# A hybrid decoder block on one core: input norm by products with a diagonal, and a norm weight that is a scale by channel

## The chip, the cores and the metric

The kernel runs on one core of a Trainium2 chip. The metric is the device time of one execution in microseconds (us). A core has five engines with an instruction stream each, which run in order and wait for each other by semaphores: TensorE (PE in the profile; its weight loads are PEld), VectorE (DVE), ScalarE (ACT), GpSimd (POOL) and SyncE (SP), which here issues nearly all transfers. Data lie in an on-chip memory of 128 partitions; TensorE's results go to eight PSUM banks of 128 x 512 float32.

## The reference

One decoder block on 512 tokens of 1024 channels, float32. Only the beginning matters here:

```
u    = rmsnorm(x, norm_mix_pre_w)        # x * rsqrt(mean(x*x) + 1e-6) * w, by token
proj = u @ w_in                          # 1024 x 10528
q, k, v, z, xbc, dt_raw, gate_logits = split(proj)
```

Then come a dilated attention on q, k and v, a Mamba-2 mixer on z, xbc and dt, projections of both that are merged by gates, an output projection, and an MLP with squared ReLU, each with residuals and norms. All of that is the same in both kernels.

## The kernel before, in words

Every large product is made of three products in a reduced float32 format: each operand is split into a high part, which ScalarE copies, and a low part, which VectorE (or GpSimd) gets by subtraction; then high x high, high x low and low x high are added up in PSUM (`three`, line 229). So a weight piece needs a transfer into `ws`, a ScalarE pass into `wh` and a VectorE or GpSimd pass into `wl` before TensorE can use it.

The start of the kernel (lines 272 to 424) makes the normed input `u`, transposed so that channels lie on partitions, in high parts `uh` and low parts `ul`, and from it the values v and the step sizes dt. x is taken in four blocks of 128 tokens (i = 0 to 3). For a block, `square_u` squares it on ScalarE with a sum by token, VectorE adds epsilon, and GpSimd takes the power of -0.5 (`rs`, one number for each token). `norm_u` multiplies x by `rs` and by the norm weight on VectorE; the weight lies in `row0`, one row that a transfer repeats over all 128 partitions. `transpose_u` turns eight 128x128 pieces on TensorE into two PSUM banks, and `split_u` makes the high and the low parts.

The values are 768 columns, taken in three groups d of 256 columns, in the order d = 1, 0, 2; group 0 has the 32 columns of dt with it and so 288. `values(d, i)` is one such group for one block: eight steps k over the channels, three products each, all into one bank `psv`; then ScalarE copies it to `vtok`. The table `V_STEPS` says what is put in behind step k of `values(d, i)`: "s" is `square_u`, "n" is `norm_u`, "t" the transposes and the split of a block, "w" the split of the weights of group 0, "p" the weights of group 2.

Most of these instructions are pinned, so they stand on their engine in the order in which the program names them. The others (the splits of later weights, the copies to `vtok`, three scalings of constants `cw`, `cb` and `bg` on GpSimd at line 400) are put among them by a scheduler. SyncE issues its transfers in the order of the program; a transfer's semaphore is used again eight transfers later, so a late issue can wait for an earlier landing. From line 425 on the order is the same in both kernels.

Of the kernel before, what the change touches and what calls it, by code (L numbers as in the profile page):

```python
# [11 lines left out]
F32 = mybir.dt.float32  # L12
F32R = mybir.dt.float32r
AF = mybir.ActivationFunctionType
ALU = mybir.AluOpType
# [3 lines left out]
P = 128  # L19
# [58 lines left out]
def hybrid_block(ctx: ExitStack, tc: tile.TileContext, a: dict):  # L78
# [193 lines left out]
    with tc.tile_pool(name="start", bufs=1, reuse_waits="tile") as st:  # L272
        VW = UC + SH
        row0 = st.tile([P, D], F32, name="row0")
        xt = st.tile([P, NT, D], F32, name="xt")
# [6 lines left out]
        def load_x(i):  # L282
            for cs in (slice(0, T), slice(T, D)) if i == 0 else (slice(0, D),):
                sp.dma_start(xt[:, i, cs], a["x"][0, i * P : (i + 1) * P, cs])

        def load_row(cs):
            sp.dma_start(row0[:, cs], a["norm_mix_pre_w"][:, cs].broadcast_to([P, T]))
# [14 lines left out]
        sp.dma_start(ws0[:, :, UC:], w_in[:, :, OFF_DT : OFF_DT + SH])  # L302
        ssq = st.tile([P, NT], F32, name="ssq")
        sq0 = st.tile([P, 2], F32, name="sq0")
        rs = st.tile([P, NT], F32, name="rs")
        uns, pts = {}, {}

        def square_u(i):
            un = uns[i] = st.tile([P, D], F32, name=f"un{i}", tag="un", bufs=2)
            if i == 0:  # L310
                for n, cs in enumerate((slice(0, T), slice(T, D))):
                    pin(act.activation(un[:, cs], xt[:, i, cs], AF.Square, scale=RD, accum_out=sq0[:, n : n + 1]))
                pin(dve.tensor_scalar(rs[:, i : i + 1], sq0[:, 0:1], sq0[:, 1:2], EPS, ALU.add, ALU.add))
            else:
                pin(act.activation(un, xt[:, i, :], AF.Square, scale=RD, accum_out=ssq[:, i : i + 1]))
                pin(dve.tensor_scalar(rs[:, i : i + 1], ssq[:, i : i + 1], EPS, None, ALU.add))
            pin(pool.tensor_tensor(rs[:, i : i + 1], rs[:, i : i + 1], mhalf, op=ALU.pow))

        def norm_u(i):
            for cs in (slice(0, T), slice(T, D)):  # L320
                pin(dve.scalar_tensor_tensor(uns[i][:, cs], xt[:, i, cs], rs[:, i : i + 1], row0[:, cs],
                                             op0=ALU.mult, op1=ALU.mult))

        def transpose_u(i, b):
            pt = pts[i, b] = abank(f"ut{i}_{b}")
            for j in range(4):
                k = 4 * b + j
                tr(pt[:, j * P : (j + 1) * P], uns[i][:, k * P : (k + 1) * P])

        def split_u(i, b):  # L330
            p3 = pts.pop((i, b)).rearrange("p (k t) -> p k t", k=4)
            hi = uh[:, 4 * b : 4 * b + 4, i * P : (i + 1) * P]
            pin(act.activation(hi, p3, AF.Copy))
            pin(dve.tensor_tensor(ul[:, 4 * b : 4 * b + 4, i * P : (i + 1) * P], p3, hi.bitcast(F32), op=ALU.subtract))

# [5 lines left out]
        def split_v0(k, eng=dve):  # L341
            ks = slice(k, k + 4)
            pin(act.activation(wh0[:, ks, :], ws0[:, ks, :], AF.Copy))
            pin(eng.tensor_tensor(wl0[:, ks, :], ws0[:, ks, :], wh0[:, ks, :].bitcast(F32), op=ALU.subtract))
# [12 lines left out]
        for j, n in enumerate(("dt_bias", "a_log")):  # L357
# [22 lines left out]

        norm_u(1)
        wv = {1: (v3(wh1, KD), v3(wl1, KD))}
        for d, i in V_ORDER:
            for k, _ in enumerate(values(d, i)):
                for step, n in V_STEPS.get((d, i, k), ()):
                    if step == "t":
                        transpose_u(n, 0)
                        transpose_u(n, 1)
                        split_u(n, 0)
                        split_u(n, 1)  # L390
                    elif step == "w":
                        split_v0(0)
                        split_v0(4, pool)
                    elif step == "p":
                        prep(0, 0)
                        wv[2] = [v3(t, KD) for t in take("v2")]
                    else:
                        (square_u if step == "s" else norm_u)(n)
        for t in (cw, cb_, bg):
# [713 lines left out]
```

## Time and profile before

| | |
|---|---|
| median of 3 runs | 1108.72 us (1108.58 to 1109.34) |
| the profiled execution | 1109.38 us, its span 1107.6 us |
| PE busy | 1089.4 us, 98% of the span |
| DVE, ACT, POOL busy | 663.0, 489.5, 63.5 us |
| first transposes, first product of the values | 7.78 us, 11.02 us |
| TensorE's idle time ahead of transposes of the input norm | 9.4 us in three waits |

Times in the rows that follow are us from the start of the span. A row of a timeline gives the start, the duration, the engine, the line of the kernel, the operation, what it writes and reads, the shape, how many instructions the row merges, and in brackets how long the engine sat idle before it and what ended that. Rows of TensorE overlap, since products are pipelined: the spacing of their starts is what one costs. In lists of waits come the time in total, the number of waits and the longest.

### The profile page before, as it was taken

To read this page: it belongs to the slowest core of one execution; us is meant where nothing else is said; L and a number is where in the kernel's file an instruction comes from. 1 tells how busy PE (TensorE), PEld (TensorE's weight loads), DVE (VectorE), ACT (ScalarE), POOL (GpSimd) and SP (SyncE) were. 2 spreads that over 40 slices of the span, in tenths; PEclk is the share of its full clock that TensorE was granted. 3 is DMA by queue.
4 is the path that set the end of the run, shared out by engine and by line. 5 is a ranking of instruction groups with operands and counts; after the bars stand their busy time and mean duration, and the time that the engine had idled before them with its cause. 6 is when DMAs were issued, how large, how long until landed. Compare 5 with 4: busy or idle time off the path is not lost.

```text
span 1107.6 us, 13600 instructions
## 1 busy us (share of the span) xinstructions
PE 1089.4 (98%) x5501; PEld 906.4 (82%) x5501; DVE 663.0 (60%) x978; ACT 489.5 (44%) x835; POOL 63.5 (6%) x71
## 2 busy tenths in 40 slices
PE   6999999999999999999999999999999999999997
PEld 5988887778878888888888888889888888888886
DVE  5657666446776869696969695865423234332324
ACT  6346656445375654637373723454322324232321
POOL 2203122000000000000000000000000000000000
PEclk9999999999999999999999999999999999999999
DMA  8232122323323232332423233540333233323212
GB/s 274 81 100 83 56 70 67 105 67 105 114 76 115 77 114 77 114 103 88 140 84 120 77 86 105 200 142 12 118 100 104 86 114 133 114 77 114 77 37 76
DMA packets 86463, 110.86 MB, mean 100 GB/s; under 512 B 4080, under 2 KB 74224, under 8 KB 85376
## 3 DMA queue, kind: packets, MB, share of 16 engines
q1 hardware_dynamic: 85072, 101.01, 28.4%
q0 software_dynamic: 1328, 8.98, 2.2%
q8 instruction: 43, 0.70, 0.3%
q14 instruction: 20, 0.16, 0.1%
HBM read 107.81 MB, written 2.16 MB: 99 GB/s over the span
## 4 chain that ended last, share of the span: by engine, by line
PE 94%; ACT 2%; DVE 2%; issue 1%; DMA 1%; SPq 0%; POOL 0%; POOLq 0%; DVEq 0%; ACTq 0%
PE psu L221 16%; PE psd L221 15%; PE psz L221 8%; PE pssp L221 8%; PE psx L221 8%; PE psbc L221 6%; PE psga L221 4%; PE psgs L221 4%; PE psk L221 3%; PE psq L221 3%; PE psv L221 3%; PE psap L221 3%; PE psp L221 2%; PE pso L221 2%; PE pq L221 1%; PE pyd L221 1%
## 5 line engine op out<-in xcount | busy, mean ns | idle before, releaser
L221 PE MATMUL psu<-fh,wh_up 128*128 128x512 f32 (+1 forms) x288 | 105.4, 366 | 0.0
L221 PE MATMUL psu<-fl,wh_up 128*128 128x512 f32 (+1 forms) x288 | 105.2, 365 | 0.0
L221 PE MATMUL psu<-fh,wl_up 128*128 128x512 f32 (+1 forms) x288 | 105.2, 365 | 0.0
L221 PE MATMUL psd<-wl_dn,hh 128*128 128x512 f32 x240 | 93.4, 389 | 0.0
L221 PE MATMUL psd<-wh_dn,hl 128*128 128x512 f32 x240 | 93.4, 389 | 0.0
L221 PE MATMUL psd<-wh_dn,hh 128*128 128x512 f32 x240 | 93.4, 389 | 0.0
L93 DVE TENSOR_TENSOR wl_up<-ws_up,wh_up 128x2048 fp32r<-128x2048 f32 x16 | 36.7, 2292 | 77.6 <-ACT wh_up L90 77.4
L93 DVE TENSOR_TENSOR hl<-hidden,hh 128x512 fp32r<-128x512 f32 x32 | 21.9, 693 | 77.3 <-ACT hh L90 77.2
L90 ACT ACTIVATE hh<-hidden 128x512 fp32r<-128x512 f32 x32 | 20.2, 632 | 103.1 <-PE psd L221 97.6
L221 PEld LDWEIGHTS psu<-fl,wh_up 128*128 128x128 f32 x288 | 54.3, 189 | 8.8
L221 PEld LDWEIGHTS psu<-fh,wh_up 128*128 128x128 f32 x288 | 54.3, 189 | 8.7
L221 PEld LDWEIGHTS psu<-fh,wl_up 128*128 128x128 f32 x288 | 54.3, 189 | 8.7
L90 ACT ACTIVATE wh_up<-ws_up 128x2048 fp32r<-128x2048 f32 x16 | 30.7, 1916 | 61.3 <-PE psu L221 56.1
L221 PE MATMUL psbc<-uh,wh_bc 128*128 128x512 f32 x128 | 52.8, 413 | 0.0
L221 PEld LDWEIGHTS psd<-wh_dn,hh 128*128 128x128 f32 x240 | 45.1, 188 | 9.5
L221 PEld LDWEIGHTS psd<-wl_dn,hh 128*128 128x128 f32 x240 | 45.1, 188 | 9.5
L221 PEld LDWEIGHTS psd<-wh_dn,hl 128*128 128x128 f32 x240 | 45.1, 188 | 9.2
L221 PE MATMUL pssp<-yth,wh_sp 128*128 128x512 f32 x128 | 51.3, 401 | 0.0
L221 PE MATMUL psz<-uh,wh_z 128*128 128x512 f32 x128 | 51.1, 399 | 0.0
L221 PE MATMUL psx<-uh,wl_x 128*128 128x512 f32 x128 | 49.9, 390 | 0.7 <-DVE wl_x L93 0.7
L221 PE MATMUL psx<-uh,wh_x 128*128 128x512 f32 x128 | 50.5, 394 | 0.0
L221 PE MATMUL psz<-uh,wl_z 128*128 128x512 f32 x128 | 50.2, 392 | 0.2 <-DVE wl_z L93 0.2
(271 smaller groups left out, 2786.1 us busy)
## 6 DMA issues: line engine op xcount, KB each, us to landing
ws_up<-in_w_up_dram SPq DMA_DIRECT2D x16, 1024.0 KB, 5.4
ws_dn<-in_w_down_dram SPq DMA_DIRECT2D x15, 1024.0 KB, 5.0
ws_z<-in_w_in_dram SPq DMA_DIRECT2D x8, 1024.0 KB, 7.3
ws_x<-in_w_in_dram SPq DMA_DIRECT2D x8, 1024.0 KB, 5.2
w<-acs_d POOLq DMA_DIRECT2D x8, 1024.0 KB, 6.1
ws_bc<-in_w_in_dram SPq DMA_DIRECT2D x16, 512.0 KB, 4.6
ws_sp<-in_w_ssm_proj_dram SPq DMA_DIRECT2D x8, 1024.0 KB, 5.0
ws_ga<-in_w_in_dram SPq DMA_DIRECT2D x4, 1024.0 KB, 5.3
```

Source lines behind the costliest of these rows:

```text
L90: ins = act.activation(hi, src, AF.Copy)
L93: ins = (eng or dve).tensor_tensor(lo, src, hi.bitcast(F32), op=ALU.subtract)
L221: tc.keep_in_program_order(pe.matmul(*args, **kw))
```

## The change

The norm weight is no longer a row on all partitions but a column: `ncol` holds it as 128 x 8, channel on partition, sent by ScalarE's queue. The transposes become true products: x itself is the stationary operand and the moving one is a diagonal of `rs` (`diag_u`, identity times `rs` by token on VectorE), so the product transposes and scales by token at once. `norm_u` is gone. The norm weight is then a scale by partition on the transposed rows: for blocks 1 to 3 and the second half of block 0 `split_u` has an added VectorE pass into `un` that multiplies by `ncol`, ahead of the high and the low part; for the first half of block 0 `split_u0` takes the channel pieces one by one and has the scale in ScalarE's copy and in VectorE's subtraction. For blocks 0 and 1 the second half of the squares is a VectorE instruction that multiplies and sums (`tensor_tensor_reduce`). Block 1 of x is sent in halves, behind the first weight piece instead of behind the last. Ahead of all stand 24 products of ones with ones into a bank that nobody reads. In the table, the squares of block 2 move from behind step 2 of the first group to behind the transposes of block 1, and the "n" steps fall away; the diagonals of blocks 2 and 3 are made right ahead of their transposes.

```diff
-V_STEPS = {(1, 0, 2): (("s", 2),), (1, 0, 5): (("t", 1),), (1, 0, 6): (("n", 2),), (1, 1, 1): (("s", 3),),
-           (1, 1, 3): (("t", 2),), (1, 1, 5): (("n", 3),), (1, 2, 3): (("t", 3), ("w", 0)), (1, 2, 7): (("p", 0),)}
+V_STEPS = {(1, 0, 5): (("t", 1), ("s", 2)), (1, 1, 1): (("s", 3),),
+           (1, 1, 3): (("t", 2),), (1, 2, 3): (("t", 3), ("w", 0)), (1, 2, 7): (("p", 0),)}
+WARM = 24
...
-        load_row(slice(0, T))
+        act.dma_start(ncol, a["norm_mix_pre_c"])
         for k in range(0, KD, 2):
             sp.dma_start(v3(ws1, KD)[:, k : k + 2, :], w_in[:, k : k + 2, OFF_V + UC : OFF_V + 2 * UC])
             if k == 0:
-                load_row(slice(T, D))
-            if k == KD - 2:
                 load_x(1)
...
         def square_u(i):
+            jk = st.tile([P, D], F32, name=f"jk{i}", tag="jk", bufs=2)
+            if i < 2:
+                pin(act.activation(jk[:, :T], xt[:, i, :T], AF.Square, scale=RD, accum_out=ssq[:, i, 0:1]))
+                pin(dve.tensor_scalar(ssq[:, i, 1:2], ssq[:, i, 0:1], EPS, None, ALU.add))
+                pin(dve.tensor_tensor_reduce(jk[:, T:], xt[:, i, T:], xt[:, i, T:], 1.0 / D, ssq[:, i, 1:2], ALU.mult,
+                                             ALU.add, rs[:, i : i + 1]))
...
+        def diag_u(i):
+            dgs[i] = st.tile([P, P], F32, name=f"dgu{i}", tag="dgu", bufs=2)
+            pin(dve.tensor_scalar(dgs[i], ident, rs[:, i : i + 1], None, ALU.mult))
+
+        def transpose_u(i, b, banks=1):
...
-                tr(pt[:, j * P : (j + 1) * P], uns[i][:, k * P : (k + 1) * P])
+                mm(pts[i, b][0][j], xt[:, i, k * P : (k + 1) * P], dgs[i], start=True, stop=True)
 
         def split_u(i, b):
...
+            pin(dve.tensor_tensor(un, p3, ncol[:, ks].unsqueeze(2).broadcast_to([P, 4, P]), op=ALU.mult))
+            hi = uh[:, ks, ts]
+            pin(act.activation(hi, un, AF.Copy))
+            pin(dve.tensor_tensor(ul[:, ks, ts], un, hi.bitcast(F32), op=ALU.subtract))
+
+        def split_u0(k):
+            pk = pts[0, 0][0][k]
+            hi = uh[:, k, 0:P]
+            pin(act.activation(hi, pk, AF.Copy, scale=ncol[:, k : k + 1]))
+            pin(dve.scalar_tensor_tensor(ul[:, k, 0:P], pk, ncol[:, k : k + 1], hi.bitcast(F32), op0=ALU.mult,
+                                         op1=ALU.subtract))
...
+        warm = gbank("warm")
+        for _ in range(WARM):
+            mm(warm[:, 0:P], ones, ones, start=True, stop=True)
         square_u(0)
-        norm_u(0)
         split_v1(0)
-        transpose_u(0, 0)
+        diag_u(0)
+        transpose_u(0, 0, 2)
         transpose_u(0, 1)
-        split_v1(2, pool)
-        split_u(0, 0)
-        split_v1(4)
+        square_u(1)
+        split_u0(0)
+        split_u0(1)
+        split_v1(2)
+        split_u0(2)
+        split_u0(3)
+        split_v1(4, pool)
         split_u(0, 1)
         split_v1(6)
-        square_u(1)
+        diag_u(1)
...
                     if step == "t":
+                        if n > 1:
+                            diag_u(n)
                         transpose_u(n, 0)
```

The order of the instructions moves at three places of which the prediction speaks. Numbers behind a name are those of the buffer; a 0 or 1 ahead of it is the half of the block. `rs` is the addition or the power, `un` the normed rows (before) or the scaled transposed half (now), `jk` what the squares leave, `dgu` the diagonal, `vtok` the copy of a finished group.

VectorE from block 1 to block 2, before:

```order
L316 TENSOR_SCALAR rs<-ssq 128x1
L321 SCALAR_TENSOR_TENSOR un_153<-xt,rs,row_98 128x512 x2
L316 TENSOR_SCALAR rs<-ssq 128x1
L334 TENSOR_TENSOR ul<-ut_0_200,uh 128x4x128
L334 TENSOR_TENSOR ul<-ut_1_205,uh 128x4x128
L321 SCALAR_TENSOR_TENSOR un_187<-xt,rs,row_98 128x512 x2
```

The same place now:

```order
L319 TENSOR_SCALAR dgu_191<-ident,rs 128x128
L333 TENSOR_TENSOR un_0_240<-ut_00_230,ncol 128x512
L336 TENSOR_TENSOR ul<-un_0_240,uh 128x4x128
L333 TENSOR_TENSOR un_1_244<-ut_10_235,ncol 128x512
L336 TENSOR_TENSOR ul<-un_1_244,uh 128x4x128
L314 TENSOR_SCALAR rs<-ssq 128x1 x2
L319 TENSOR_SCALAR dgu_276<-ident,rs 128x128
```

The addition for block 2 stood ahead of block 1's low parts; now the additions for blocks 2 and 3 stand together behind them, and block 2's diagonal behind both.

ScalarE at the same place, before:

```order
L315 ACTIVATE un_153,ssq<-xt 128x1024
L315 ACTIVATE un_187,ssq<-xt 128x1024
L333 ACTIVATE uh<-ut_0_200 128x4x128
L333 ACTIVATE uh<-ut_1_205 128x4x128
L377 ACTIVATE vtok<-psv_0_177 128x256
L315 ACTIVATE un_230,ssq<-xt 128x1024
```

And now:

```order
L335 ACTIVATE uh<-un_0_240 128x4x128
L438 ACTIVATE rows<-rows 128x32
L393 ACTIVATE vtok<-psv_0_211 128x256
L335 ACTIVATE uh<-un_1_244 128x4x128
L313 ACTIVATE jk_248,ssq<-xt 128x1024
L313 ACTIVATE jk_266,ssq<-xt 128x1024
L335 ACTIVATE uh<-un_0_288 128x4x128
```

The squares of blocks 1 and 2 stood ahead of block 1's high parts and those of block 3 behind them; now the squares of blocks 2 and 3 both stand behind the two high parts of block 1 and the copy of the first group.

GpSimd from the first power on, before:

```order
L317 TENSOR_TENSOR rs<-rs,mhalf 128x1
L339 TENSOR_TENSOR wl_v_109<-ws_v_107,wh_v_108 128x512
L317 TENSOR_TENSOR rs<-rs,mhalf 128x1 x3
L400 TENSOR_SCALAR cw<-cw 128x128
L400 TENSOR_SCALAR cb<-cb 128x32
L400 TENSOR_SCALAR bg<-bg 128x16
L344 TENSOR_TENSOR wl_v_102<-ws_v_100,wh_v_101 128x1152
```

And now:

```order
L315 TENSOR_TENSOR rs<-rs,mhalf 128x1 x2
L348 TENSOR_TENSOR wl_v_109<-ws_v_107,wh_v_108 128x512
L417 TENSOR_SCALAR cw<-cw 128x128
L417 TENSOR_SCALAR cb<-cb 128x32
L315 TENSOR_TENSOR rs<-rs,mhalf 128x1
L417 TENSOR_SCALAR bg<-bg 128x16
L315 TENSOR_TENSOR rs<-rs,mhalf 128x1
L353 TENSOR_TENSOR wl_v_102<-ws_v_100,wh_v_101 128x1152
```

All four powers stood ahead of the scalings of the constants; now `cw` and `cb` are scaled ahead of block 2's power, and `bg` ahead of block 3's.

VectorE between blocks 2 and 3 now (before, the two halves of `wl_v` of group 2 stood behind all low parts of block 3):

```order
L333 TENSOR_TENSOR un_0_288<-ut_00_278,ncol 128x512
L336 TENSOR_TENSOR ul<-un_0_288,uh 128x4x128
L333 TENSOR_TENSOR un_1_292<-ut_10_283,ncol 128x512
L95 TENSOR_TENSOR wl_v_361<-ws_v_358,wh_v_360 128x1024
L336 TENSOR_TENSOR ul<-un_1_292,uh 128x4x128
L319 TENSOR_SCALAR dgu_322<-ident,rs 128x128
L95 TENSOR_TENSOR wl_v_361<-ws_v_358,wh_v_360 128x1024
```

One half of group 2's low part is now ahead of block 2's last low part and of block 3's diagonal, the other right behind that diagonal. ScalarE's two high halves of that weight have moved with them.

More of the change, by code (lines that the diff above doesn't have):

```diff
@@ L273, in hybrid_block @@
         VW = UC + SH
-        row0 = st.tile([P, D], F32, name="row0")
+        ncol = st.tile([P, KD], F32, name="ncol")
         xt = st.tile([P, NT, D], F32, name="xt")
@@ L282, in load_x @@
         def load_x(i):
-            for cs in (slice(0, T), slice(T, D)) if i == 0 else (slice(0, D),):
+            for cs in (slice(0, T), slice(T, D)) if i < 2 else (slice(0, D),):
                 sp.dma_start(xt[:, i, cs], a["x"][0, i * P : (i + 1) * P, cs])
-        def load_row(cs):
-            sp.dma_start(row0[:, cs], a["norm_mix_pre_w"][:, cs].broadcast_to([P, T]))
         load_x(0)
@@ L302, in hybrid_block @@
         sp.dma_start(ws0[:, :, UC:], w_in[:, :, OFF_DT : OFF_DT + SH])
-        ssq = st.tile([P, NT], F32, name="ssq")
-        sq0 = st.tile([P, 2], F32, name="sq0")
+        ssq = st.tile([P, NT, 2], F32, name="ssq")
         rs = st.tile([P, NT], F32, name="rs")
-        uns, pts = {}, {}
+        pts, dgs = {}, {}
         def square_u(i):
[L309 to L313, printed above, removed]
-            else:
-                pin(act.activation(un, xt[:, i, :], AF.Square, scale=RD, accum_out=ssq[:, i : i + 1]))
-                pin(dve.tensor_scalar(rs[:, i : i + 1], ssq[:, i : i + 1], EPS, None, ALU.add))
+            jk = st.tile([P, D], F32, name=f"jk{i}", tag="jk", bufs=2)
[4 more added lines that the diff above has]
+                                             ALU.add, rs[:, i : i + 1]))
+            else:
+                pin(act.activation(jk, xt[:, i, :], AF.Square, scale=RD, accum_out=ssq[:, i, 0:1]))
+                pin(dve.tensor_scalar(rs[:, i : i + 1], ssq[:, i, 0:1], EPS, None, ALU.add))
@@ L326, in transpose_u @@
+        def transpose_u(i, b, banks=1):
+            pt = [abank(f"ut{i}_{b}{n}") for n in range(banks)]
+            pts[i, b] = [pt[j % banks][:, j * P : (j + 1) * P] for j in range(4)], pt[0]
             for j in range(4):
                 k = 4 * b + j
-                tr(pt[:, j * P : (j + 1) * P], uns[i][:, k * P : (k + 1) * P])
+                mm(pts[i, b][0][j], xt[:, i, k * P : (k + 1) * P], dgs[i], start=True, stop=True)
         def split_u(i, b):
-            p3 = pts.pop((i, b)).rearrange("p (k t) -> p k t", k=4)
@@ L397, in hybrid_block @@
                     else:
-                        (square_u if step == "s" else norm_u)(n)
+                        square_u(n)
         for t in (cw, cb_, bg):
@@ L1096 @@
     data["conv_b"] = data["conv_b"][0].reshape(32, P).T
+    data["norm_mix_pre_c"] = data["norm_mix_pre_w"][0].reshape(8, P).T
     data["b_gate"] = data["b_gate"][0].reshape(16, P).T
```

13 lines of the change are left out of this document (3 added, 10 removed).

## The prediction

> **What bounds the kernel now.** I read the page first, then the list of waits of TensorE, then the timeline of each engine over the first 32 us.
>
> ```profile
> span 1107.6 us, 13600 instructions
> PE 1089.4 (98%) x5501; PEld 906.4 (82%) x5501; DVE 663.0 (60%) x978; ACT 489.5 (44%) x835; POOL 63.5 (6%) x71
> PEclk9999999999999999999999999999999999999999
> ```
> ```profile
> PE ut L224 <- DVE un L321: 9.4, 3, 7.8
> PE pyd L221 <- DVE w L764: 0.8, 2, 0.6
> PE psx L221 <- DVE wl_x L93: 0.7, 1, 0.7
> PE rg L221 <- ACT dg L819: 0.6, 1, 0.6
> ```
>
> TensorE (PE) is the bound: 1089.4 of 1107.6 us. The waits worth naming sum to 11.5 us, and 9.4 of them are the three before transposes of the input norm, which is what is changed. So whatever the start loses or gains reaches the end of the kernel: behind it only 2.1 us of waits are left that could swallow a delay.
>
> ```profile
> 7.78 1.11 PE L224 MATMUL ut<-ident,un 128*128 128x128 f32 x4 [7.78 <-DVE un L321]
> 9.97 1.12 PE L224 MATMUL ut<-ident,un 128*128 128x128 f32 x4 [1.08 <-DVE un L321]
> 11.02 0.58 PE L221 MATMUL psv<-wh_v,uh 128*128 128x256 f32 x1
> 13.40 0.41 PE L221 MATMUL psv<-wh_v,uh 128*128 128x256 f32 x1
> 13.62 0.41 PE L221 MATMUL psv<-wl_v,uh 128*128 128x256 f32 x1
> 14.29 0.28 PE L221 MATMUL psv<-wh_v,ul 128*128 128x256 f32 x1
> 14.41 0.28 PE L221 MATMUL psv<-wh_v,uh 128*128 128x256 f32 x1
> 15.51 1.23 PE L224 MATMUL ut<-ident,un 128*128 128x128 f32 x8 [0.58 <-DVE un L321]
> 18.86 0.40 PE L224 MATMUL ut<-ident,un 128*128 128x128 f32 x2
> 22.91 1.04 PE L224 MATMUL ut<-ident,un 128*128 128x128 f32 x8
> 28.09 0.30 PE L221 MATMUL psv<-wh_v,uh 128*128 128x288 f32 x1
> 31.28 0.30 PE L221 MATMUL psv<-wh_v,uh 128*128 128x288 f32 x1
> ```
>
> These are the marks of TensorE's start: transposes of row block 0 (in two batches), 1, 2 and 3 at 7.78, 15.51, 18.86 and 22.91; the first value product with 288 columns at 28.09, the next block's at 31.28. The spacing of products falls from 0.22 us (13.40 to 13.62) to 0.12 (14.29 to 14.41): the clock comes up about 14.0, some 3.0 us after the first product and 4.1 after the second batch of transposes. The page's row of the granted clock reads 9 in every slice and shows nothing of this.
>
> **The change, leg by leg.** Prices first.
>
> ```profile
> 3.91 0.63 ACT L312 ACTIVATE un<-xt 128x512 f32<-128x512 f32 x1 [1.90 <-DMA xt<-in_x_dram]
> 7.57 0.63 ACT L338 ACTIVATE wh_v<-ws_v 128x512 fp32r<-128x512 f32 x1 [2.30 <-DMA ws_v<-in_w_in_dram]
> 13.95 1.06 ACT L315 ACTIVATE un<-xt 128x1024 f32<-128x1024 f32 x1 [0.20 <-DVE rs L316]
> 14.91 0.19 ACT L315 ACTIVATION_READ_ACCUMULATOR un<-xt 128x1 f32 x1
> 16.18 1.19 ACT L333 ACTIVATE uh<-ut 128x512 fp32r<-128x512 f32 x2 [1.08 <-PE ut L224]
> 26.89 2.01 ACT L90 ACTIVATE wh_v<-ws_v 128x1024 fp32r<-128x1024 f32 x2
> 24.52 2.23 ACT L343 ACTIVATE wh_v<-ws_v 128x1152 fp32r<-128x1152 f32 x2
> ```
> ```profile
> 9.16 0.75 DVE L321 SCALAR_TENSOR_TENSOR un<-xt,rs,row 128x512 f32<-128x512 f32 x1 [1.44 <-DMA row<-in_norm_mix_pre_w_dram]
> 16.81 1.29 DVE L334 TENSOR_TENSOR ul<-ut,uh 128x512 fp32r<-128x512 f32 x2 [0.72 <-ACT uh L333]
> 31.76 2.35 DVE L93 TENSOR_TENSOR wl_q<-ws_q,wh_q 128x1024 fp32r<-128x1024 f32 x2
> 43.86 0.29 DVE L412 TENSOR_TENSOR dt<-dt,dt 128x128 f32<-128x128 f32 x1
> ```
> ```profile
> 10.56 1.28 POOL L339 TENSOR_TENSOR wl_v<-ws_v,wh_v 128x512 fp32r<-128x512 f32 x1 [4.33 <-ACT wh_v L338]
> 14.02 0.56 POOL L317 TENSOR_TENSOR rs<-rs,mhalf 128x1 f32<-128x1 f32 x1 [2.19 <-DVE rs L316]
> 21.55 1.05 POOL L400 TENSOR_SCALAR cw<-cw 128x128 f32<-128x128 f32 x1 [1.44 <-DMA cw<-in_conv_w_dram]
> 22.59 0.47 POOL L400 TENSOR_SCALAR cb<-cb 128x32 f32<-128x32 f32 x1
> 26.82 2.80 POOL L344 TENSOR_TENSOR wl_v<-ws_v,wh_v 128x1152 fp32r<-128x1152 f32 x1 [3.55 <-ACT wh_v L343]
> ```
> ```profile
> 277.75 1.06 PE L221 MATMUL pcb<-ct,ct 128*128 128x128 f32 x8
> 278.56 0.48 PE L221 MATMUL psap<-ah,wh_ap 128*128 128x512 f32 x1
> ```
>
> A 128x512 pass costs 0.65 us on VectorE (1.29 for two) and 0.6 on ScalarE (1.19 for two); a square of 1024 columns with its readout 1.15 (13.95 to 15.10); the power on GpSimd 0.56; a 128x128 VectorE pass 0.29, which I take for the pieces of block 0, and 0.25 for the diagonal. A true f32 product of 128x128 fills two rows of the trace: the four of pcb take 0.81 us, 0.2 each, while the eight transposes of block 3 take about 0.8 (0.1 each). Eight products with a diagonal so cost 1.6 us. From transposes at 15.51 to ScalarE's copy of the first four at 16.18 are 0.67 us, of which 0.4 is work: 0.25 for the hand-over.
>
> *To the products of block 1.* The broadcast rows, for which VectorE waited until 9.16, leave SyncE's queue, and block 1 of x moves up from behind the weights. The weight piece that landed by 7.57 was fourth in the queue, now third; I estimate 5.6 (x is there at 3.91). Its high and low parts then end about 6.9, and the diagonal behind them about 7.2. The 24 warm-up products start once the ones are set, near 1.2: at 0.36 to 0.41 each until the clock rises 3.0 to 4.1 us later, then at 0.2, they end at 7.6 to 8.4; I take 8.0. So block 0's products run 8.0 to 9.6, and the first value product starts 1.4 us earlier than at 11.02. Then VectorE sets the pace: the third product has closed the first bank at 8.6, hand-over 0.25, ScalarE's piece 0.3, and from 9.2 four small low parts (1.2), one weight piece (0.65), the scaled copy (0.65), ScalarE's high part meanwhile (0.6), the low part (0.65), the last weight piece (0.65), the diagonal (0.25), and 0.4 of hand-overs: 14.2. Block 1's products start there, 1.3 us earlier than 15.51.
>
> *Block 1 to block 2.* Here is the loss. ScalarE squares block 2 and block 3 behind both copies of block 1, both copies wait for a scaled copy on VectorE, and VectorE has both additions ahead of block 2's diagonal. From the start S of block 1's products: first four done S+1.05; scale 0.65, high 0.6, low 0.65, scale 0.65, high 0.6; two squares 2.3; addition 0.2; diagonal 0.25; hand-overs 0.1: S+7.05 or 21.25. TensorE has only 1.6 + 0.7 + 1.4 us of work meanwhile and 0.7 of waiting on the low part, so it idles near 2.8 us. Before, the squares were done ahead and the distance was 3.35. There is a second gate: GpSimd now scales cw and cb ahead of block 2's power. cw came at 21.55; half a megabyte less ahead of it at some 300 GB/s makes that 19.8, and 1.05 + 0.47 + 0.56 + 0.3 for the diagonal give 22.2. Bounds: 21.25 where cw is early, 23.95 where it is as late as before. I take 22.2, 3.3 later than 18.86.
>
> *Block 2 to block 3.* First four done 23.25; scale, high, low, scale end 25.85. ScalarE's vtok of block 1 ends there too, then comes half of the next weight's high part (1.0, 26.9) ahead of the second high part; VectorE takes that weight's low half (1.2, 28.1), the low part (0.65) and the diagonal (0.25) with hand-overs: 29.1, against 22.91, 6.2 later. It holds if the weight is there by 25.9; before, ScalarE began it at 26.89 with no wait for a transfer.
>
> *Block 3 to the 288-column products.* VectorE has the other low half first (1.2, 30.3), then scale, low, scale, low with ScalarE's high parts between (3.85): 34.2. The fifth step of block 3 needs that; eleven products at 0.12 follow: 35.45 against 28.09, 7.35 later. ScalarE starts the first value weight's high halves after its last copy at 33.45; 2.2 us later, at 35.7, GpSimd starts its low half: 38.5. The products that need it are the last eleven of the first unit (0.133 each): 40.05 against 31.28, **8.8 us later**. From there the orders agree, and weights have time.
>
> Sum: the profiled 1109.38 us + 8.8 = 1118.2; it lies 0.66 over the median, so **1117.5 us**. What the reader might expect to matter does not: with products at a transpose's price the sum is 8.5, since TensorE waits anyway; a warm-up that ends at 9.9 makes it 9.5 to 10. I cost the ncol transfer and the ones at nothing: ScalarE is idle until 3.91.
>
> **Rivals.**
>
> *Only the start counts (faster).* If VectorE and ScalarE hold the four blocks' pace, that is if block 1's chain fits into 3.35 us instead of 7.05, the 1.3 us earlier products of block 1 stay: 1107.4 us. For it: the pace of the transposes before. Against it: squares alone are 2.3 of the 7.05. It decides from the point where two scaled copies and two squares take under 1 us together. 6 in 100.
>
> *Loss and gain cancel.* The chain costs only the start's 1.3 us: 1108.7. It needs the weights' halves to be out of the way, against the order in which the engines hold them. 4 in 100.
>
> *The clock falls again.* TensorE idles some 3.7 us before block 2's products (18.5 to 22.2) and 2.5 before block 3's. If the clock drops there, the next 3.0 to 4.1 us run at half speed and cost 1.5 to 2 us: 1119 to 1121. Nothing in this trace shows how long an idle stretch it takes; the longest after the clock's rise, 0.58 us, did not lower it. 14 in 100, with cw as late as before (1119.3) in it. [...]
>
> *The warm-up does nothing.* If products of ones do not raise the clock, 24 at 0.4 end at 10.9 and block 0's cost 3.2: the first value product would be at 14.1, 4.5 later than forecast, and 3.6 of it reach the end (the chains behind move with it, and the gate of cw hides 0.9): 1121 us. 6 in 100.
>
> **How the numbers follow.** The forecast holds 70 in 100; its own range, from the bounds of the terms, is 1115 to 1119.5. Rivals above it hold 20, those below 10. The range of 8 in 10 reaches up to the clock's fall, and down to half the loss (two of the four legs mis-sized): 1113 to 1121. A change of 0.2% (2.2 us) is what can be told from none: faster 6, same 4, slower 90 in 100.
>
> **What would show it.** TensorE's waits on VectorE's diagonal: about 2.5 to 4 us before block 2's products, about 2.3 before block 3's; products of block 1 at 14.2, of block 2 at 22.2, of block 3 at 29; the first 288-column product near 35.5. ScalarE's two squares of 1024 columns stand one after the other at 18.5. GpSimd's second-to-last power starts straight behind cb. I am wrong if TensorE has no wait over 1 us behind block 1's products, or if the second half of the kernel, from 32 us on, changes its own length by more than 1 us.

## The result, and the profile after

The changed kernel takes 1119.92 us (median of 5 runs, 1119.37 to 1120.19); the kernel before, run beside it, 1108.72 (1108.58 to 1109.43). The ratio is 1.0098, with a 95% interval of 1.0084 to 1.0113: 11 us, or 1.0%, slower. The forecast was 1117.5 in a range of 1113 to 1121. (Two of the five runs of experiment 3 below took 1469.28 and 2190.79 us at a mean granted clock of 0.705 and 0.942; they count in no ratio.)

The page of the changed kernel, its first lines:

```profile
span 1118.1 us, 13775 instructions
...
PE 1101.6 (99%) x5581; PEld 918.0 (82%) x5581; DVE 664.9 (59%) x988; ACT 489.6 (44%) x836; POOL 62.7 (6%) x71
...
PEclk9999999999999999999999999999999999999999
```

TensorE reads 12 us busier (1089.4 before) and its share rises to 99%. That does not show that the loss is work that had to be done: the 48 records of the warm-up count as busy, and so do products that stretch at a low clock (block 2's take 2.77 us, block 1's 2.05). The row of the granted clock reads 9 throughout, as it did before; a slice is 28 us long and hides what shorter stretches show below.

TensorE's list of waits, first 45 us:

```profile
PE ut L223 <- DVE dgu L319: 2.3, 1, 2.3
PE ut L223 <- issue: 2.1, 1, 2.1
```

The one wait of 7.8 us at the start is gone, and two new ones of 2.3 and 2.1 us stand ahead of the products of blocks 2 and 3 ("issue" means that the profile names nothing that ended the second; block 3's diagonal, below, ends 0.1 us ahead of it). TensorE's timeline (start, duration, what; in brackets the idle time before and what ended it):

```profile
1.16 8.06 PE L223 MATMUL warm<-ones 128*128 128x128 f32 x48 [1.16 <-POOL ones L214]
...
9.05 1.95 PE L223 MATMUL ut<-dgu,xt 128*128 128x128 f32 x16
...
15.15 2.05 PE L223 MATMUL ut<-dgu,xt 128*128 128x128 f32 x16
...
22.21 2.77 PE L223 MATMUL ut<-dgu,xt 128*128 128x128 f32 x16 [2.27 <-DVE dgu L319]
...
30.78 2.02 PE L223 MATMUL ut<-dgu,xt 128*128 128x128 f32 x16 [2.10 <-issue]
...
37.37 0.30 PE L223 MATMUL psv<-wh_v,uh 128*128 128x288 f32 x1
...
41.89 0.29 PE L223 MATMUL psv<-wh_v,uh 128*128 128x288 f32 x1
```

The two last rows are the starts of the first and the second *unit*, that is of the 288 columns of block 0 and of block 1. Blocks 1, 2 and 3 stood at 15.51, 18.86 and 22.91 before, the first 288-column product at 28.09, the second unit at 31.28. Now they stand at 15.15, 22.21, 30.78, 37.37 and 41.89. The second unit is 10.61 us late, the span 10.5 longer; from the second unit to the end both kernels take the same (1107.6 - 31.28 = 1076.3 and 1118.1 - 41.89 = 1076.2). The whole loss arises between 15 and 42 us: block 1 starts 0.36 us *earlier* than before.

What holds blocks 2 and 3 is read in the timelines of ScalarE, VectorE and GpSimd, one after the other:

```profile
19.61 1.04 ACT L313 ACTIVATE jk<-xt 128x1024 f32<-128x1024 f32 x1
...
20.64 1.04 ACT L313 ACTIVATE jk<-xt 128x1024 f32<-128x1024 f32 x1
...
27.29 0.38 ACT L393 ACTIVATE vtok<-psv 128x256 f32<-128x256 f32 x1 [2.52 <-PE psv L223]
...
27.57 1.05 ACT L92 ACTIVATE wh_v<-ws_v 128x1024 fp32r<-128x1024 f32 x1
```
```profile
21.81 0.15 DVE L314 TENSOR_SCALAR rs<-ssq 128x1 f32<-128x1 f32 x1 [0.89 <-ACT jk L313]
...
21.88 0.28 DVE L319 TENSOR_SCALAR dgu<-ident,rs 128x128 f32<-128x128 f32 x1
...
28.65 1.23 DVE L95 TENSOR_TENSOR wl_v<-ws_v,wh_v 128x1024 fp32r<-128x1024 f32 x1 [2.56 <-ACT wh_v L92]
...
30.40 0.28 DVE L319 TENSOR_SCALAR dgu<-ident,rs 128x128 f32<-128x128 f32 x1
```
```profile
18.89 0.54 POOL L417 TENSOR_SCALAR cw<-cw 128x128 f32<-128x128 f32 x1 [5.43 <-DMA cw<-in_conv_w_dram]
...
21.01 0.57 POOL L315 TENSOR_TENSOR rs<-rs,mhalf 128x1 f32<-128x1 f32 x1 [1.33 <-DVE rs L314]
```

The squares of blocks 2 and 3 (L313) stand one behind the other on ScalarE, after the last copy of block 1. Block 2's square ends at 20.74 with its readout; then come the addition, the power on GpSimd (21.01 to 21.58) and, at 21.88, the diagonal on VectorE; TensorE's products follow at 22.21. VectorE has the addition for *block 3* ahead of that diagonal and waits 0.89 us for its square, but most of this wait is covered by the power: it costs the diagonal at most 0.3 us (21.58 to 21.88).

Block 3's diagonal (30.40) stands behind a weight's low half (28.65), which waits for a high half on ScalarE (27.57), which stands behind `vtok` of block 1 (27.29), which waited 2.52 us for TensorE. And TensorE was late there, because it ran at half its clock (granted 0.50, below).

The trace's records of the clock have it fall at 23.36 and rise at 26.77. Three stretches of the changed kernel, parted at these times, by the view of windows (length, busy time and instructions of TensorE, its weight loads, VectorE, ScalarE and GpSimd; the third number from the end is the granted clock):

```profile
19.95:23.36 3.41, 1.15 (x10) 1.15 (x11) 0.98 (x4) 1.83 (x4) 1.38 (x3) 1.00 1.08 365
23.36:26.77 3.41, 3.41 (x19) 3.41 (x18) 1.98 (x3) 0.63 (x1) 0.00 (x0) 0.50 0.64 202
26.77:30.18 3.41, 1.91 (x16) 1.71 (x15) 1.53 (x2) 2.79 (x4) 0.00 (x0) 1.00 0.00 0
```

About one microsecond after the wait of 2.27 us, the clock falls to half and stays there for 3.4 us. Behind the second wait, of 2.10 us, it does not. The fall is not one of the profiled execution alone: the mean granted clock over the span is 0.997 in all five runs of the change, and 0.998 to 1.000 in every run of the kernel before that has it on record.

### The profile page after: what moved, and what is told of

The parts are those of the page before. It is cut to its first block, busy times and chain, and to the rows that moved or that the text cites. A ratio compares the mean times of both kernels' runs of the same rounds, so it can differ in the third digit from the quotient of the medians.

```text
span 1118.1 us, 13775 instructions
## 1 busy us (share of the span) xinstructions
PE 1101.6 (99%) x5581; PEld 918.0 (82%) x5581; DVE 664.9 (59%) x988; ACT 489.6 (44%) x836; POOL 62.7 (6%) x71
## 4 chain that ended last, share of the span: by engine, by line
PE 94%; ACT 2%; DVE 2%; issue 1%; POOL 1%; POOLq 0%; DVEq 0%; ACTq 0%
PE psu L223 16%; PE psd L223 15%; PE psz L223 8%; PE pssp L223 8%; PE psx L223 8%; PE psbc L223 6%; PE psga L223 4%; PE psgs L223 4%; PE psk L223 3%; PE psq L223 3%; PE psap L223 3%; PE psv L223 3%; PE psp L223 2%; PE pso L223 2%; PE pq L223 1%; PE pyd L223 1%
```

## The experiments

The theory after the result: (a) the order on ScalarE and VectorE makes the two waits; (b) a wait makes the clock fall; (c) warm-up and the price of a product with a diagonal matter little. The rival to (a) is the price of the products, the rival to (b) that VectorE and ScalarE set the pace there anyway. Each time of "before" below is that of runs in the same job.

**1. The two squares early, ahead of block 1's copies.**

```diff
-V_STEPS = {(1, 0, 5): (("t", 1), ("s", 2)), (1, 1, 1): (("s", 3),),
+V_STEPS = {(1, 0, 2): (("s", 2),), (1, 0, 3): (("s", 3),), (1, 0, 5): (("t", 1),),
```

> The changed kernel with the squares of blocks 2 and 3 put where ScalarE is idle, behind the last weight piece of block 0 (steps 2 and 3 of the first group), nothing else. Theory (the order of the squares holds up the chain from block 1 to block 2, and the idle time there lets the clock fall): block 2's products start near 20.7 instead of 22.21, TensorE's spacing stays at 0.12 us behind them, the weight's halves fall behind block 3's diagonal, the first 288-column product comes about 4 us earlier, and the kernel takes about 1116.2 us (1115.5 to 1117.5), 3.7 below the changed one. Rival (the added VectorE pass and the true products set the pace, not the order): under 1 us is gained, 1119 to 1120.

Measured: 1115.55 us (1115.38 to 1115.82), 1.0058 times the kernel before (1.0045 to 1.0070). TensorE's timeline of this kernel:

```profile
20.40 2.05 PE L223 MATMUL ut<-dgu,xt 128*128 128x128 f32 x16 [0.73 <-DVE dgu L319]
...
25.96 2.02 PE L223 MATMUL ut<-dgu,xt 128*128 128x128 f32 x16 [0.65 <-issue]
...
32.91 0.30 PE L223 MATMUL psv<-wh_v,uh 128*128 128x288 f32 x1
```

This change of the order, in one table, gives back 4.4 of the 11 us (1.0058 instead of 1.0098), as expected. Both waits shrink to 0.7 us, and the granted clock is 1.00 in every stretch from 8 to 38 us: with the waits, the fall is gone too. The scheduler also puts the weight's low half behind block 3's diagonal now (25.92 behind 25.58 on VectorE), so the 4.4 us hold three things. The legs from block 1 to the first unit are 18.0 us in sum (14.87 to 32.91), against 20.95 at full clock with the old order (14.31 to 35.26 in experiment 3): about 2.9 us are the order, with the weight's place, and the rest the fall.

**2. The clock kept through the first wait.** Ten products of ones into an unused bank, ahead of block 2's products.

```diff
+                        if n == 2:
+                            for _ in range(KEEP):
+                                mm(keep[:, 0:P], ones, ones, start=True, stop=True)
                         transpose_u(n, 0)
```

> The changed kernel with ten more products of ones into the bank of the warm-up, right ahead of block 2's products, so that TensorE has work in the 2.3 us in which it waits; they end before the diagonal is there. Theory (the fall of the clock behind that wait costs time of its own, because the copy of the second group and the weight's halves queue behind slow products): granted clock 1.00 throughout, block 2's eight products take 1.7 instead of 2.4 us, block 3's start near 29.1 instead of 30.78, and the kernel takes about 1118.3 us, 1.6 less. Rival (the slow stretch lies under the chain of VectorE and ScalarE and costs nothing): 1119.9.

Measured: 1119.6 us (1118.22 to 1120.25), ratio 1.0092 (1.0079 to 1.0106): not to be told from the change itself, and over the expectation. TensorE's timeline and its clock in this kernel:

```profile
29.17 2.92 PE L224 MATMUL ut<-dgu,xt 128*128 128x128 f32 x16 [2.09 <-issue]
```
```profile
29.17:30.20 1.03, 1.03 (x9) 1.03 (x10) 1.03 (x1) 0.00 (x0) 0.00 (x0) 0.95 0.00 0
30.20:33.60 3.40, 3.40 (x18) 3.40 (x18) 1.99 (x4) 0.63 (x1) 0.00 (x0) 0.51 0.65 198
```

Block 2's products kept their clock (2.05 us long at 22.16) and block 3's came 1.6 us earlier, as expected. But the wait ahead of block 3 was still there, and now the clock fell behind *it*, for 3.4 us again. The loss had moved by one block: the first unit started at 37.21, against 37.37.

**3. The clock kept through both waits.** As 2, with ten more ahead of block 3's products, into a bank of their own.

```diff
-                        if n == 2:
+                        if n > 1:
+                            kp = keep if n == 2 else abank("keep")
                             for _ in range(KEEP):
-                                mm(keep[:, 0:P], ones, ones, start=True, stop=True)
+                                mm(kp[:, 0:P], ones, ones, start=True, stop=True)
```

> The changed kernel with 10 extra products of ones by ones (each two records, some 2.1 us at full clock) ahead of block 2's products, as in the run before that one kept the clock there, and 10 more ahead of block 3's. With the first ten alone, the clock fell in block 3's products instead (granted 0.50 to 0.55 from 30 to 32 us) and the time stayed at 1119.6. Theory: the two waits of 2.1 to 2.3 us are what the clock falls on, and the fall costs what block 2's leg was longer than forecast; then no stretch up to 40 us is granted below 0.9, block 3's products start at 29.1 to 29.5 us, the first product of 288 columns at 35.9 to 36.3 us instead of 37.4, and the time is 1118.3 to 1118.7. Rival: the clock falls at a third place (before the value products that wait for ScalarE), or the fall has no part in the sum because VectorE and ScalarE set the pace there; then the product of 288 columns starts at 37.0 or later and the time is 1119.5 to 1120.

Measured: 1117.97, 1118.33 and 1119.01 us; ratio 1.0083 (1.0068 to 1.0098). The timeline and the clock:

```profile
1.16 7.22 PE L224 MATMUL warm<-ones 128*128 128x128 f32 x48 [1.16 <-POOL ones L215]
...
21.65 2.05 PE L224 MATMUL ut<-dgu,xt 128*128 128x128 f32 x16 [0.31 <-DVE dgu L320]
...
28.66 2.02 PE L224 MATMUL ut<-dgu,xt 128*128 128x128 f32 x16
...
35.26 0.30 PE L224 MATMUL psv<-wh_v,uh 128*128 128x288 f32 x1
...
39.78 0.29 PE L224 MATMUL psv<-wh_v,uh 128*128 128x288 f32 x1
```
```profile
20.00:26.00 6.00, 5.69 (x49) 5.50 (x49) 2.51 (x6) 2.40 (x5) 2.05 (x5) 1.00 0.89 295
26.00:32.00 6.00, 6.00 (x54) 5.98 (x54) 4.63 (x7) 2.60 (x4) 0.00 (x0) 1.00 0.18 41
```

At full clock throughout, the second unit starts at 39.78 instead of 41.89, and the span is 1116.2 instead of 1118.1. Of the 2.11 us, 1.56 lie between blocks 2 and 3 (7.01 us apart instead of 8.57): that is the price of the fall. The other 0.55 had arisen ahead of block 2: this execution's warm-up took 7.22 us instead of 8.06, which is also why block 3 and the first unit stand earlier than expected, and 0.28 of that was lost again on the leg to block 2. The rival to (b) falls. The time itself cannot tell this kernel from the changed one with certainty, since the intervals overlap; the leg does.

**4. The weight halves of group 2 pinned behind block 3's parts.**

```diff
-split(stage[:, f], hi[:, f], lo[:, f], eng, pinned=key == "o1", lo_pinned=lo_pinned)
+split(stage[:, f], hi[:, f], lo[:, f], eng, pinned=key in ("o1", "v2"), lo_pinned=lo_pinned or key == "v2")
```

> The changed kernel with the split of the third group's weights pinned in the order of the program, behind block 3's low parts, on ScalarE and VectorE. Theory (the scheduler's place for these halves, ahead of block 2's last low part and block 3's diagonal, delays block 3): block 2's products at 22.2 as before, block 3's near 28.5 instead of 30.78, the first 288-column product near 35.0, the kernel about 1117.9 us, 2.0 less. Rival (block 3 waits for block 2's low parts anyway): no gain, 1119.9.

Measured: 1118.0 us (1117.05 to 1118.38), ratio 1.0077 (1.0063 to 1.0091), as expected, though its interval overlaps the change's too. The wait ahead of block 2 is the same 2.27 us and the clock falls there again (0.50 from 22.0 to 25.4), but block 3 follows 7.06 us behind block 2 although the clock fell: the weight's low half no longer stands between `vtok`, which the fall delays, and block 3's diagonal. Either way out shortens the same leg, from 8.57 to 7.06 here and to 7.01 in experiment 3; together they were tried only in 6, with more edits.

**5. A shorter warm-up: 18 products instead of 24.**

> The changed kernel with 18 instead of 24 warm-up products. Theory (block 0's products stood behind the warm-up, which ended at 9.05, while the diagonal was there at 7.94): they start near 8.0, and all of it reaches the end: about 1119.0 us, 0.9 less. Rival (block 1's products wait for weights or for VectorE as late as now): 1119.9; the clock's rise could also come later, then 1120.

Measured: 1120.63 us (1120.0 to 1121.96), ratio 1.0105 (1.0091 to 1.0119): a miss of 1.6. Block 0's products started at 7.93, as expected, and block 1's at 14.03, 1.1 us earlier, but the leg to block 2 grew from 7.06 to 7.42 and the fall was longer. On that leg the constant `cw` landed late, at 19.75 instead of 18.89, GpSimd's power for block 2 stood straight behind `cb`, and VectorE waited 0.28 us for it. The windows of this kernel:

```profile
16.99:20.40 3.41, 1.59 (x12) 1.25 (x10) 1.76 (x4) 2.68 (x5) 0.65 (x2) 1.00 0.91 234
20.40:23.81 3.41, 2.36 (x11) 2.36 (x12) 0.69 (x3) 0.25 (x2) 1.45 (x4) 0.50 1.07 358
23.81:27.23 3.42, 3.42 (x18) 3.42 (x18) 1.74 (x3) 0.63 (x1) 0.00 (x0) 0.50 0.33 107
```

The clock fell while TensorE still waited (18.81 to 21.45), at 20.40, and rose at 27.23: 6.83 us, twice the 3.41. The wait was 2.64 us long, hardly longer than the 2.27 of the changed kernel. A gain at the start was eaten behind it; the last section sets the two waits side by side.

**6. The order mended as a whole.** The squares early; the diagonals of blocks 2 and 3 right behind block 1's scaled copies; of each block first both scaled copies, then both low parts; the weight of group 2 behind. Products, warm-up and norm are as in the change. A part of the edit:

```diff
+            for b in range(2):
+                ...
+                pin(dve.tensor_tensor(un, p3, ncol[:, ks].unsqueeze(2).broadcast_to([P, 4, P]), op=ALU.mult))
+                pin(act.activation(uh[:, ks, ts], un, AF.Copy))
+                uns.append(un)
+            if i == 1:
+                diag_u(2)
+                diag_u(3)
+            for b in range(2):
+                ...
+                pin(dve.tensor_tensor(ul[:, ks, ts], uns[b], uh[:, ks, ts].bitcast(F32), op=ALU.subtract))
```

> The changed kernel with its order mended: squares of blocks 2 and 3 early, their diagonals right behind block 1's scaled copies, in each block both scaled copies ahead of both low parts, and the third group's weights behind block 3. The work is the same. Theory (the order lost the time; what then stays is the price of the products with a diagonal, 1.75 against 0.85 us for each block on TensorE, and a short wait for a low part): block 2's products some 5.3 us after block 1's, block 3's 4.8 after those, no idle stretch over 1.3 us, granted clock 1.00; 3.6 us more than the kernel before, about 1112.5. Rival (the added VectorE pass is the bound, whatever the order): no gain over the run with the squares early, 6 us more than before.

Measured: 1112.51 us (1112.4 to 1113.57), ratio 1.0033 (1.0021 to 1.0044), as expected. The timeline:

```profile
14.63 2.05 PE L223 MATMUL ut<-dgu,xt 128*128 128x128 f32 x16
...
19.74 1.95 PE L223 MATMUL ut<-dgu,xt 128*128 128x128 f32 x16
...
24.40 1.95 PE L223 MATMUL ut<-dgu,xt 128*128 128x128 f32 x16
...
30.50 0.30 PE L223 MATMUL psv<-wh_v,uh 128*128 128x288 f32 x1
```

The waits ahead of blocks 2 and 3 are gone. The order, with the fall that it brings about, is worth 7.2 of the 11 us (from 1.0098 to 1.0033).

**7. As 6, with transposes in blocks 1 to 3.** These blocks are turned by the identity instead of the diagonal, so the scale by token is left out there: the kernel does less than the reference asks, and its time serves only to price the products.

```diff
+                if i:
+                    tr(pts[i, b][0][j], xt[:, i, k * P : (k + 1) * P])
+                else:
```

> The run with the mended order, with transposes by the identity in place of the products with a diagonal in blocks 1 to 3; so these three blocks lack the scale by token. The diagonals are still made. Theory (true products cost 0.9 us of TensorE for each block, and TensorE is the bound there): about 3.3 us less than the mended order, 1109.2, near the kernel before. Rival (VectorE's chain is the bound): under 1 us less.

Measured: 1111.0 us (1110.11 to 1111.52), ratio 1.0016 (1.0007 to 1.0025): 1.5 us less than 6 by the medians, 1.9 by the ratios, where 3.3 were expected. The timeline:

```profile
14.95 1.04 PE L226 MATMUL ut<-ident,xt 128*128 128x128 f32 x8
...
17.69 0.39 PE L223 MATMUL psv<-wh_v,uh 128*128 128x256 f32 x1 [0.99 <-ACT uh L349]
...
19.91 1.04 PE L226 MATMUL ut<-ident,xt 128*128 128x128 f32 x8
...
23.98 1.04 PE L226 MATMUL ut<-ident,xt 128*128 128x128 f32 x8
...
29.48 0.30 PE L223 MATMUL psv<-wh_v,uh 128*128 128x288 f32 x1
```

From block 1 to block 2 hardly anything is won (4.96 us against 5.11): TensorE waits 0.99 us for a high part instead. From 2 to 3 and from 3 to the 288 columns it is 0.6 us each (4.07 and 5.50, against 4.66 and 6.10). So part of the products' price stays hidden even in the well-ordered kernel: VectorE and ScalarE set the step from block 1 to 2.

**8. As 6, without the warm-up.**

```diff
-WARM = 24
+WARM = 0
```

> The run with the mended order, without the warm-up products. Theory (the warm-up delays block 0's products as much as it speeds them, and VectorE's chain from block 0 to block 1 sets the pace behind them): block 0's products start near 8.0 and take 3.5 us at 0.44 each; block 1's products come within 0.5 us of where they are with the warm-up; the time is within 1 us of that run. Rival (a cold start costs what it looks like, 1.8 us in block 0's products and 1.2 in the value products): 3 us more.

Measured: 1112.84 us (1112.09 to 1113.19), ratio 1.0032 (1.0019 to 1.0044), the same as with it. The timeline of TensorE, with one row of ScalarE:

```profile
6.64 3.79 PE L223 MATMUL ut<-dgu,xt 128*128 128x128 f32 x16 [6.64 <-DVE dgu L319]
...
16.69 0.23 ACT L452 ACTIVATE rows<-rows 128x32 f32<-128x32 f32 x1 [1.94 <-DMA rows<-in_a_log_dram]
...
30.26 0.30 PE L223 MATMUL psv<-wh_v,uh 128*128 128x288 f32 x1
```

Without the warm-up block 0's products start at 6.64, when the diagonal is ready, and take twice their time (3.79 us instead of 1.95); with it they run at full speed, but behind the warm-up, at 8.53 there. The two do not balance at once: block 1's products start at 13.73 without the warm-up and at 14.63 with it, 0.90 us apart, where at most 0.5 was expected. The lead then shrinks to 0.24 at block 2 (19.50 against 19.74), since ScalarE, in its order, waits until 16.69 for a transfer of constants (`a_log`) ahead of block 1's high parts, and TensorE waits 1.00 us for these. In experiment 6 that row of ScalarE stands behind the first high part. So the equal times do not show that a cold start costs nothing; whether the 0.9 us would last without that wait, no run shows.

**9. The kernel before, with 18 warm-up products ahead of its transposes.** This asks whether a warm start helps at all.

> The kernel before with 18 warm-up products ahead of the input norm and nothing else. Theory (block 1's transposes at 15.51 wait for x, the square and the normed rows, not for TensorE): block 1's transposes stay at 15.5, so nothing is gained; the products ahead of them end earlier, TensorE idles some 2 us there, and the clock may fall: the time of the kernel before, or up to 1.5 us more. Rival (the cold products before are on the path): 1.3 us less.

Measured: 1109.15 us (1108.48 to 1109.66), ratio 1.0000 (0.9991 to 1.0009). TensorE's timeline and its clock:

```profile
9.63 0.66 PE L224 MATMUL ut<-ident,un 128*128 128x128 f32 x4 [1.63 <-DVE un L321]
```
```profile
10.00:12.00 2.00, 1.41 (x8) 0.97 (x7) 1.54 (x4) 2.00 (x5) 1.27 (x1) 0.83 1.03 407
12.00:14.00 2.00, 2.00 (x11) 2.00 (x11) 1.37 (x4) 1.68 (x4) 0.32 (x1) 0.50 1.03 386
```

The warm-up did raise the clock (the four transposes in this row take 0.66 us, in the kernel before 1.12), and it fell again, at 11.34, behind the wait of 1.63 us and one of 0.37 after it: it is at half where the value products run.

**10. The start of the change on the kernel before.** Block 0 alone by diagonal and weight by channel, no warm-up, the broadcast row loaded behind the first weight pieces, block 1's x and squares in halves as in the change; blocks 1 to 3 scaled by token and row and transposed, as before. A part of the edit:

```diff
-        norm_u(0)
-        transpose_u(0, 0)
-        transpose_u(0, 1)
+        pin(dve.tensor_scalar(dgu, ident, rs[:, 0:1], None, ALU.mult))
+        products_0(0, 2)
+        products_0(1, 1)
+        square_u(1)
+        split_u0(0)
+        split_u0(1)
```

> The kernel before with the diagonal and the weight by channel for block 0 alone, no warm-up products, and the weight's row, which blocks 1 to 3 still use, loaded behind the weight pieces of the first products; blocks 1 to 3 are scaled by token and row and transposed as before. Theory: what the change wins is the start, since block 0 needs no row and no pass over its 1024 columns before TensorE; what it loses is the pace of blocks 1 to 3. Taken alone the first wins: block 1's transposes at 14.6 to 14.9 us instead of 15.5, the rest follows at the legs of the kernel before (3.3, 4.1 and 5.2 us, 288-column product at 27.4 to 27.8 instead of 28.1 or so), and the time is 0.5 to 0.9 us under the kernel before, 1108.2 to 1108.7. Rival: the chain on VectorE and ScalarE from block 1 on sets block 2's start whatever block 0 does, or the row comes late behind the weight pieces; then block 2's transposes start no earlier than before and the time is 1109 to 1110.5.

Measured: 1108.95 us (1108.51 to 1110.74, 11 runs), ratio 1.0000 (0.9991 to 1.0009). The timeline:

```profile
14.78 1.03 PE L224 MATMUL ut<-ident,un 128*128 128x128 f32 x8
...
18.08 1.29 PE L224 MATMUL ut<-ident,un 128*128 128x128 f32 x8
...
27.43 0.30 PE L221 MATMUL psv<-wh_v,uh 128*128 128x288 f32 x1
```

In the profiled execution the marks are 0.7 to 0.8 us earlier than before, as expected, and its span 0.6 shorter (1107.0). The times miss the expectation (1108.2 to 1108.7): nothing shows in them, and a gain of 0.6 us lies within the interval, so it is neither shown nor excluded. Nothing tried here beats the kernel before by more than can be measured.

**What the 11 us are made of**, going back from the change to the kernel before (ratios as multiples of the time before, 1109 us):

| step | ratio | worth |
| --- | --- | --- |
| the change | 1.0098 | |
| order mended (6): squares, diagonals, low parts, weight halves; no fall of the clock | 1.0033 | 7.2 us |
| transposes for the products in blocks 1 to 3 (7) | 1.0016 | 1.9 us |
| left against the kernel before | 1.0000 | 1.8 us |

What is left: in experiment 7 the step from block 1 to block 2 still takes 4.96 us, with the scaling behind the transposes and both copies of a block on VectorE and ScalarE, where the kernel before took 3.35 with rows that were scaled ahead. This last reading is argued from the timeline; no run isolates it, and the last row holds what the products of block 0 and the start bring as well.

## Why the prediction was right, and where it was off

The direction, the mechanism and the range of 1113 to 1121 held; the result lies just over the forecast's own range (1115 to 1119.5), and the profiled execution came out at 1119.85 us, 1.7 over the 1118.2 of the sum. Leg by leg on TensorE, forecast and measured:

| leg | forecast | measured | full clock (3) |
| --- | --- | --- | --- |
| start to block 1 | 14.2 | 15.15 | 14.31 |
| block 1 to 2 | 8.0 | 7.06 | 7.34 |
| block 2 to 3 | 6.9 | 8.57 | 7.01 |
| block 3 to 288 columns | 6.35 | 6.59 | 6.60 |
| the first unit | 4.6 | 4.52 | 4.52 |
| second unit at | 40.05 | 41.89 | 39.78 |

*What bounds it* held: the tail behind 42 us kept its length within 0.2 us, and no wait there swallowed the delay.

*To the products of block 1* was 0.95 short. The step that failed is the end of the warm-up, taken at 8.0 from a range of 7.6 to 8.4 (its own prices give 7.3 to 8.1); block 0's products follow it at 9.05. The first 23 of its 48 records stand 0.21 us apart, so a product took 0.43 us instead of 0.36 to 0.41, and the clock rose at 6.29, 5.1 us after the first, instead of 3.0 to 4.1. The prediction's own bound ("a warm-up that ends at 9.9 makes it 9.5 to 10") had named the sign. Over the executions the same 24 products took from 7.22 to 8.07 us, with the rise at 4.54 to 6.31; not one of them had ended by 8.0.

*Block 1 to block 2* held by the first chain, S+7.05 against 7.06, squares one after the other and all. What failed is the second gate, which I took to bind (22.2, or 8.0 after block 1). By GpSimd's rows above, `cw` came at 18.89, 0.9 earlier than my 19.8, and its scaling took 0.54 instead of 1.05; GpSimd then waited 1.33 us for VectorE. The two misses of 0.95 cancel, so block 2 stood at 22.21 against 22.2 by luck. The gate can bind: in experiments 3 and 5 `cw` came at 19.95 and 19.75, the power stood straight behind `cb`, VectorE waited 0.18 and 0.28 us for it, and the leg was 7.34 and 7.42 us. Among the change and experiments 2 to 5, `cw` came between 18.28 (experiment 2) and 19.95.

*Block 2 to block 3* is the term that was mis-sized: 6.9 forecast, 8.57 measured, 7.01 with the clock kept. The rival "the clock falls again" came true on top of the forecast, at 1.56 us, within the 1.5 to 2 that it was given, and in the range of time (1119 to 1121) that it named. It stood at 14 in 100 because no row before showed such a gap (the longest after the rise was not 0.58 us, as the prediction has it, but the 0.7 ahead of `psx` in its own list). It happened at an idle stretch of 2.27 us. In the runs, falls came behind waits of 2.09 (experiment 2), 2.27 (the change and 4), 2.64 (5) and, with 0.37 after it, 1.63 us (9).

*What was said not to matter*: "with products at a transpose's price the sum is 8.5", that is 0.3 us. The changed kernel itself wasn't tried with transposes. In the mended order they bring 1.5 to 1.9 us, since TensorE no longer waits there; hidden costs come back when the cover is taken away.

*The rivals below.* That only the start counts fell with block 2; that loss and gain cancel, too. That the warm-up does nothing is half true: it does raise the clock (block 0's products took 1.95 us with it in experiment 6, 3.79 without it in 8), but in the times of experiments 8 and 9 it is worth nothing; in 9 the clock falls again before the value products, and by 8 it delays block 0's products.

## What to carry to other kernels

When work moves from ahead of TensorE to behind it, follow each engine's order to the next block: here two squares that stand behind two copies instead of ahead of them cost 4.4 us with the fall that they led to, and mending the order as a whole gave back 7.2 of 11. In the changed kernel a gap of 2.27 us on TensorE cost more than itself, another 1.56 us by the clock, while behind one of 2.10 us the clock stayed at 1.00; so look at the granted clock over stretches of 1 to 3 us, since the page's 40 slices hide it. A warm-up that ends after the first work is ready delays that work (the change: block 0's diagonal was there at 7.94, its products started at 9.05), and in experiment 9 the clock fell again behind waits of 1.63 and 0.37 us that followed the warm-up; neither won anything here.

## What the runs showed that I had not expected

The clock fell behind waits of TensorE of 1.63 to 2.64 us, but not behind every one: the wait of 2.10 ahead of block 3 passed without, in the changed kernel and in experiment 5, and waits of 0.65 to 0.99 us (experiments 1 and 7) did. Where it fell, it fell up to 1.7 us after work had resumed (9) or, in experiment 5, while the wait lasted, and it stayed at half for 3.41 us (the change, 2, 4, 9) or 6.83 (5).

The records of the clock give the times. In the changed kernel the clock changes at 6.29, 23.36 and 26.77, so 17.07 and 3.41 us apart; in experiment 5 at 6.75, 20.40 and 27.23, 13.65 and 6.83 us apart; in 9 at 4.51, 11.34 and 14.75, 6.83 and 3.41 us apart. By the windows shown for the changed kernel, the 3.41 us ahead of the fall (19.95 to 23.36) hold 2.26 us in which TensorE idles, the wait of 2.27; the 3.41 us from the rise on (26.77 to 30.18) hold 1.50, all but 0.60 of the wait of 2.10, and the clock stays at 1.00. By those of experiment 5, the 3.41 us ahead of the fall (16.99 to 20.40) hold 1.82 us of idle time; the next, at half clock, hold 1.05, the rest of its wait, and the 3.42 after them none; then the clock rises. So of two waits of nearly the same length in one kernel, 2.27 and 2.10 us, one went with a fall and the other did not. What sets them apart is not shown: no run moves a wait from one place to another.

The granted clock does not show the cold start: in the changed kernel it reads 1.00 from 2 to 6 us, where a warm-up product takes 0.43 us, twice the 0.21 of a product with the diagonal at 9.05 (16 records in 1.71 us). The trace's first record of the clock is the rise at 6.29, and the view reads 1.00 ahead of it, so only the spacing of the records tells. A fall in the middle shows in both.
